# Values by matmuls of 512 columns, and the AdaLN rows' loads moved ahead in a hybrid decoder layer

## The chip, the core and the metric

The kernel runs on one core of a Trainium2 chip. The metric is the device time of one execution in microseconds. Engines are named as in the profile: PE (TensorE) with its weight loads PEld, DVE (VectorE), ACT (ScalarE), POOL (GpSimd) and SP (SyncE, which issues most DMAs here).

## The reference

One decoder layer, one sequence of 512 tokens, width 2048, in float32. A mixing layer runs two groups of heads side by side: stick-breaking attention with 8 heads of 128, and an RG-LRU recurrence with 8 heads of 128; then comes a squared-ReLU MLP of width 8192. Each of the two sub-layers is normalised and modulated by six vectors (shift, scale and gate twice) that come from the conditioning vector c.

```python
mod = silu(c) @ w_ada + b_ada            # six vectors of 2048
h   = rmsnorm(x, g) * (1 + scale) + shift
q, k, v, xr, xg = split(h @ w_in)        # 3 x 1024 and 2 x 1024 columns
z = q k^T * 128**-0.5                    # per head, strictly causal
A[t,s] = sigmoid(z_ts) * prod_(s<j<t) (1 - sigmoid(z_tj))
attn = A v
lru  = scan(a, u) * gelu(xg)             # a, u from sigmoid gates of conv(xr)
x = x + gate * (concat(rmsnorm(attn), rmsnorm(lru)) @ w_out)
x = x + gate * (relu(h2 @ w_mlp_in)**2 @ w_mlp_out)
```

The names here are shortened; the sums are those of the reference.

## The kernel before, in words

Activations lie transposed: 16 chunks k of 128 features by 512 tokens. Every product is made from two halves of each operand, a high part in the reduced format fp32r and the rest: `mm3` issues high x high, low x high and high x low (L259, L262, L263) into one PSUM bank of 128x512. Weights come in by SP (L236, tile `wr`), ACT rounds them to the high part (L244, `wh`) and DVE subtracts (L122, `wl`). There are eight PSUM banks: four `mm`, three `z`, one `o`.

The stages that matter, in order of time:

- The first query-key group is fused with the first V group (from about 105 to 200 us): for each k, 12 matmuls of 128x512 into the `mm` banks and the V matmuls of heads 0 to 3 (`v_mm`, L470 to L472) into the `z` and `o` banks. For V the tokens are the stationary operand, a block of 128 at a time, and the weights are the moving one.
- `qk_group(2)`, then `v_group(4)` (V of heads 4 to 7 into the `mm` banks, about 256 to 317 us), `qk_group(4)` and `qk_group(6)`, then `xg_group(0)`, the first half of the recurrence's gate input (from about 436 us).
- Between their matmuls, generators put pieces of other work: `pair(h)` is attention for heads h and h + 1 (scores, the shares of the stick with two triangular constants at L652, values), `gates` and `scans` are the recurrence (L587 to L595: exponential and square on ACT, sums, roots on ACT, product and a scan on DVE), and `adas` builds the modulation vectors: DVE multiplies a row of w_ada by c and sums it (L211), from an `x` buffer that SP has loaded (L199), and L220 adds bias. Each `yield` gives its spacing in units of the main stream, and `pace` is 3.2 or 1.6 for a row of `adas`.

All instructions are put into one order per engine when the kernel is built, by a scheduler with priorities; an engine then works through its own list without leaving it. A tile that is asked for while its pool is full gets the buffer of an older one, and its first writer waits for the last reader of that.

Two pools matter. `x` has 4 buffers, for AdaLN rows, for the recurrence's temporaries and the gates' operands. `a` has 64 buffers of 128x512, for the normalised activations (two for each of 16 chunks), for the query and key halves, the V halves, the attention outputs and the recurrence's streams `xr_t` and `conv_y`. The evictions of query-key banks (`qk_evac`, ACT at L459, then DVE at L460) and of V banks (`v_evac`, L480 and L481) take two `a` buffers a bank. They are asked for with high priority. The heads' parts of a V bank are read by `values` through the table `vt`; the two buffers of a bank come free when the last of those parts has been read.

Of the kernel before, what the change touches and what calls it, by code (L numbers as in the profile page):

```python
# [12 lines left out]
AF = mybir.ActivationFunctionType  # L13
ALU = mybir.AluOpType
PSUM = bass.MemoryType.PSUM

P = 128
S = 512
D = 2048
NK = D // P  # L20
# [44 lines left out]
def hybrid_layer_kernel(  # L65
# [32 lines left out]
    def T(tag, dt=F32, cols=None):  # L98
        return new(next(split_tag) if tag == "w4" else tag, dt, cols)
# [13 lines left out]
    act = nc.scalar.activation  # L113
    stt = nc.vector.scalar_tensor_tensor
    tt = nc.vector.tensor_tensor
    mm = nc.tensor.matmul

    def f32(ap):
        return ap.bitcast(F32)
# [104 lines left out]
    rows, rows2 = Rows(SC1, SH1), Rows(GT1, SC2, SH2)  # L224
    MID = itertools.cycle(["x"])
# [4 lines left out]
    def weights(src, tag=None, urgent=URGENT, pin=False):  # L230

        n = src.shape[-1] if len(src.shape) == 2 else src.shape[1] * src.shape[2]
        with tc.high_priority(offset=urgent):
            r = T("wr" if tag not in ("w3", "w4", "ts") else "raw")
            dst = r[:, :n] if len(src.shape) == 2 else r[:, :n].rearrange("p (a b) -> p a b", b=src.shape[2])
            dma = nc.sync.dma_start(dst, src)  # L236
            if pin:
                later(dma)
            if tag in ("w4", "ts"):
                both = T(tag, F32R)  # L240
                h, lo = both[:, :S], both[:, S : 2 * S]
            else:
                h, lo = T(tag or "wh", F32R), T(tag or "wl", F32R)
            act(h[:, :n], r[:, :n], AF.Copy)  # L244
            low(lo[:, :n], r[:, :n], h[:, :n])
        return h, lo
# [18 lines left out]
    def blk(o):  # L265
        return slice(o * P, (o + 1) * P)
# [32 lines left out]
    bg, bgl, bg2 = Lane(), Lane(), Lane()  # L299
# [67 lines left out]
    xs, xhl, hT = {}, {}, {}  # L367
# [35 lines left out]
    def weights1(k, halves=(0, 1)):  # L403
        return [weights(w_in[blk(k), XR + i * 512 : XR + (i + 1) * 512], tag="a", urgent=min(k * 28, URGENT), pin=True) for i in halves]
# [6 lines left out]
    w = weights1(0, [0])  # L411
# [4 lines left out]
    for k in range(NK):  # L416
# [18 lines left out]
        for hf in range(2):  # L435
            wh, wl = w[hf]
            for o in range(4):
                mm3(banks[hf * 4 + o], wh[:, blk(o)], wl[:, blk(o)], *xhl[k], k == 0, k == NK - 1)
        w = w_next
    xr_t = []  # L440
    for o in range(8):
        t = T("a")
# [5 lines left out]
    qk, vt, o_t = {}, {}, []  # L448
# [13 lines left out]

    def v_mm(bs, w, k, os=range(4)):

        ah, al = hT[k]
        for o, b in ((o, b) for o in os for b in (o % 2 * 2, o % 2 * 2 + 1)):
            wh, wl = (t[:, o // 2 * 256 : o // 2 * 256 + 256] for t in w)
            out = bs[o][:, (b % 2) * 256 : (b % 2) * 256 + 256]
            st = k == 0 and b % 2 == 0
            mm(out, ah[:, blk(b)], wh, start=st, stop=False, skip_group_check=True)  # L470
            mm(out, al[:, blk(b)], wh, start=False, stop=False, skip_group_check=True)
            mm(out, ah[:, blk(b)], wl, start=False, stop=k == NK - 1, skip_group_check=True)  # L472

    def v_evac(bs, h0, os=range(4)):

        for o in os:
            p, b = o // 2, o % 2
            h, lo = T("a", F32R), T("a", F32R)
            with tc.high_priority(offset=EVAC):
                act(h, bs[o], AF.Copy)  # L480
                tt(out=lo, in0=bs[o], in1=f32(h), op=ALU.subtract)  # L481
            for j in range(2):
                for hd in range(2):
                    c = slice(j * 256 + hd * P, j * 256 + (hd + 1) * P)
                    vt[(h0 + 2 * p + hd, 2 * b + j)] = (h[:, c], lo[:, c])


    banks = [bank(t) for t in BANKS]
    for k in range(NK):
        if k + 2 < NK:  # L490
            prep2(k + 2)
        wh, wl = weights(src_qk[blk(k), :, : 2 * P])
        for o in range(4):
            mm3(banks[o], wh[:, blk(o)], wl[:, blk(o)], *hT[k], k == 0, k == NK - 1)
        v_mm(banks[4:], weights(src_v(k, 0, 4)), k)
    qk_evac(banks[:4], 0)
    v_evac(banks[4:], 0)

    def qk_group(h0, begun=(0, None)):
# [3 lines left out]
    def v_group(h0):  # L503
        bs = [bank("mm") for _ in range(4)]
        load, step = lambda k: weights(src_v(k, h0, 4)), lambda k, w, os: v_mm(bs, w, k, os)
        for k in range(NK - 2):
            step(k, load(k), range(4))
            tick()
        ending(load, step, range(NK - 2, NK), lambda o: v_evac(bs, h0, [o]))
# [88 lines left out]
    def lru_out(o0):  # L598
        for o in range(o0, o0 + 4):
            act(xg_t[o], xg_t[o], AF.Gelu_apprx_tanh)  # L600
        yield 1.0
        for o in range(o0, o0 + 4):
            g = xg_t[o]
            tt(out=g, in0=conv_y[o], in1=g, op=ALU.mult)
            add_square(acc_l, g, T("n"), o == 0)
            yield 1.0
# [89 lines left out]
    def adas(m):  # L696
        for j in range(NK):
            if tags2[0] is MID:
                rows2.row(m, j, MID)
                yield pace[0]  # L700
            else:
                for q in range(2):
                    rows2.row(m, j, LATE, q)
                    yield pace[0] / 2
        ready.add(m)

    pace = [3.2]
# [26 lines left out]
    def xg_group(o0, tags):  # L734
        bs = [bank(t) for t in tags]

        def evac(b):
            t = T("a")
            copy(b, t, bs[b])
            xg_t[o0 + b] = t  # L740

        group(bs, range(NK), lambda k: w_in[blk(k), XG + o0 * P : XG + (o0 + 4) * P], lambda k: hT[k], evac)
# [4 lines left out]
    bg.drain()  # L747
    bg.add(pair(2))
    bg2.add(adas(GT1), adas(SC2), adas(SH2))
    v_group(4)  # L750
    bg.drain()
# [14 lines left out]
    bg.add(attn_mix())  # L766
    bgl.add(lru_out(0))
    tags2[0] = LATE
    rows2.load(5, LATE)
    xg_group(4, BANKS[4:])  # L770
    bg.drain()
# [46 lines left out]
    def out_evac(outs, g, tok, held=None):  # L818
# [35 lines left out]
        out=gm2, in0=mods[:, SC2 * NK : (SC2 + 1) * NK], scalar=1.0, in1=vec[:, C_GMLP : C_GMLP + NK],  # L854
# [226 lines left out]
    def strassen(src, acts, after=None, pre=None, before=None, js=range(8)):  # L1081

        bs = [bank(next(turn)) for _ in PRODUCTS]
        if pre:
            n, ts = pre
            with tc.high_priority(offset=SETE):
                for b, t in zip(bs, ts):
                    act(b, t, AF.Copy)
                for b, t in zip(bs[5:], load_pre(n, (5, 6), nc.scalar)):
                    act(b, t, AF.Copy)  # L1090
        if before:
            loaded[0] = before()
        for j in js:
            w, a = operands(src(j)), acts(j)
            for b, (an, wn) in zip(bs, PRODUCTS):
                (ah, al), (wh, wl) = a[an], w[wn]
                for i in range(2):
                    out, st = b[:, q_(i)], j == js[0] and i == 0 and not pre
                    kw = dict(skip_group_check=True)
                    mm(out, wh[:, blk(i)], ah, start=st, stop=False, **kw)  # L1100
                    mm(out, wh[:, blk(i)], al, start=False, stop=False, **kw)  # L1101
                    mm(out, wl[:, blk(i)], ah, start=False, stop=j == js[-1], **kw)  # L1102
            if after:
                after(j)
            tick()
        return bs
# [108 lines left out]
    for g in range(1, NG):  # L1215
# [3 lines left out]
        bs = strassen(lambda j: w_pair[j][:, :, g * 512 : (g + 1) * 512], acts_in, last, js=range(KP)[:: -1 if g == 1 else 1])  # L1219
# [35 lines left out]
    for i, (n, ps) in enumerate(parts):  # L1255
# [15 lines left out]
        bs = strassen(src, acts_out, after, nxt, before, ps)  # L1271
        nxt = loaded[0]
        if n not in left:
# [11 lines left out]
            with tc.high_priority(offset=SETW):  # L1285
                for k, tok, q in quarters(n, *qs):
                    t = x2[k][:, tok]
# [5 lines left out]
        else:  # L1293
            with tc.high_priority(offset=SETE):
                for j, b in enumerate(bs):
                    t = T("a")
# [14 lines left out]
    for p in final:  # L1311
        t = T("a", F32R)
# [154 lines left out]
```

## Time and profile before

| | us |
|---|---|
| median of 3 runs | 2001.72 (1998.12 to 2003.39) |
| the profiled execution | 2001.01 |
| its span, first to last instruction | 1999.3 |
| PE busy | 1947.6 (97%) |
| DVE busy | 1761.3 (88%) |
| ACT busy | 1073.4 (54%) |

The mean granted clock is 0.995. A matmul's busy time in the profile (0.28 us for 256 columns, 0.40 for 512) is longer than its step to the next start, since matmuls are pipelined; its cost in a stream is the distance of starts. In a timeline row stand the start, the duration, the engine, the line, the operation, the written and the read tile, the sizes, and in brackets the idle time before it with what ended it. A row of waits names the engine, tile and line that waited, whom it waited for, the total, the number of waits and the longest.

### The profile page before, as it was taken

How to read it: one execution, taken by the hardware profiler on the slowest of the kernel's cores; microseconds unless marked ns; L12 is line 12 of the kernel's file. 1: busy time of each engine (PE TensorE's matmuls, PEld its weight loads, DVE VectorE, ACT ScalarE, POOL GpSimd, SP SyncE). 2: the span in 40 equal slices, each digit the busy share in tenths (PEclk: the TensorE clock that was granted, in tenths of full speed). 3: DMA queues.
4: the chain of work that ended last, by engine and by line, in shares of the span. 5: the costliest groups of instructions: out<-in, count | busy, mean ns of one | idle time of the engine just before them, and what ended most of it. 6: DMA issues, size and time to landing. Idle time of an engine off the chain costs nothing. (4 is left out here: it accounts for less than half of the span.)

```text
span 1999.3 us, 37951 instructions
## 1 busy us (share of the span) xinstructions
PE 1947.6 (97%) x14532; PEld 1836.1 (92%) x14532; DVE 1761.3 (88%) x2971; ACT 1073.4 (54%) x1572; POOL 193.6 (10%) x307
## 2 busy tenths in 40 slices
PE   8999999999999998999999999999999999999997
PEld 6789898788888898999999999999999999999996
DVE  8998786888998599999999999999879879878996
ACT  5443564786533386555556555555445645556552
POOL 0000000000000000111211211200110210211100
PEclk9999999999999999999999999999999999999998
DMA  9896655646779543766766765756567668679653
GB/s 365 305 319 213 201 169 183 188 140 213 228 251 362 183 144 113 236 211 196 227 201 191 227 204 187 232 170 219 190 232 270 226 246 287 215 253 346 225 196 111
DMA packets 205241, 443.56 MB, mean 222 GB/s; under 512 B 20481, under 2 KB 42113, under 8 KB 205058
## 3 DMA queue, kind: packets, MB, share of 16 engines
q1 hardware_dynamic: 176338, 356.58, 54.3%
q0 software_dynamic: 23680, 77.61, 10.4%
q10 hardware_dynamic: 5040, 6.93, 1.0%
q8 instruction: 114, 1.87, 0.4%
q14 instruction: 69, 0.57, 0.1%
HBM read 376.30 MB, written 64.75 MB: 221 GB/s over the span
## 5 line engine op out<-in xcount | busy, mean ns | idle before, releaser
L1100 PE MATMUL ps_mm<-a,w 128*128 128x256 f32 x1696 | 468.3, 277 | 3.0 <-DVE a L1112 1.2
L1102 PE MATMUL ps_mm<-a,w 128*128 128x256 f32 x1696 | 468.5, 277 | 0.4 <-DVE w L122 0.3
L1101 PE MATMUL ps_mm<-a,w 128*128 128x256 f32 x1696 | 468.3, 276 | 0.3 <-DVE a L122 0.3
L1070 ACT ACTIVATE w<-ts 128x1024 fp32r<-128x1024 f32 x244 | 258.4, 1059 | 276.2 <-DVE ts L1066 246.5
L1102 PE MATMUL ps_z<-a,w 128*128 128x256 f32 x1304 | 361.6, 278 | 7.0 <-DVE w L122 6.7
L1100 PE MATMUL ps_z<-a,w 128*128 128x256 f32 x1304 | 361.6, 278 | 3.8 <-DVE a L1116 1.7
L1101 PE MATMUL ps_z<-a,w 128*128 128x256 f32 x1304 | 360.9, 277 | 0.1
L122 DVE TENSOR_TENSOR w<-ts,w 128x1024 fp32r<-128x1024 f32 x244 | 298.4, 1223 | 54.7 <-PE ps_mm L1101 17.7
L1100 PEld LDWEIGHTS ps_mm<-a,w 128*128 128x128 f32 x1696 | 318.3, 188 | 4.3 <-issue 2.6
L1102 PEld LDWEIGHTS ps_mm<-a,w 128*128 128x128 f32 x1696 | 318.4, 188 | 1.2 <-DVE w L122 1.0
L1101 PEld LDWEIGHTS ps_mm<-a,w 128*128 128x128 f32 x1696 | 318.5, 188 | 0.7 <-DVE a L122 0.7
L122 DVE TENSOR_TENSOR w<-raw,w 128x768 fp32r<-128x768 f32 (+1 forms) x296 | 268.5, 908 | 37.1 <-ACT w L244 21.8
L1064 ACT ACTIVATE w<-raw 128x768 fp32r<-128x768 f32 x244 | 204.4, 838 | 168.4 <-issue 77.2
L1102 PEld LDWEIGHTS ps_z<-a,w 128*128 128x128 f32 x1304 | 245.6, 189 | 8.4 <-DVE w L122 8.3
L1100 PEld LDWEIGHTS ps_z<-a,w 128*128 128x128 f32 x1304 | 245.6, 188 | 5.4 <-issue 2.2
L1101 PEld LDWEIGHTS ps_z<-a,w 128*128 128x128 f32 x1304 | 245.6, 188 | 0.6 <-DVE a L122 0.6
L244 ACT ACTIVATE wh<-wr 128x512 fp32r<-128x512 f32 (+1 forms) x184 | 113.1, 618 | 151.3 <-PE ps_mm L262 62.4
L1058 DVE TENSOR_TENSOR ts<-raw 128x512 f32<-128x512 f32 x244 | 167.6, 688 | 14.1 <-DMA raw<-in_w_mlp_out_dram 13.6
L259 PE MATMUL ps_mm<-a,wh 128*128 128x512 f32 x448 | 176.3, 394 | 3.8 <-ACT wh L244 2.2
L263 PE MATMUL ps_mm<-a,wl 128*128 128x512 f32 x448 | 175.4, 392 | 0.8 <-DVE wl L122 0.6
L262 PE MATMUL ps_mm<-a,wh 128*128 128x512 f32 x448 | 174.8, 390 | 0.0
L211 DVE SCALAR_TENSOR_TENSOR x<-x,cb 128x1024 f32<-128x1024 f32 x108 | 131.8, 1224 | 25.0 <-DMA x<-in_w_adaT_dram 24.9
(336 smaller groups left out, 4156.7 us busy)
## 6 DMA issues: line engine op xcount, KB each, us to landing
raw<-in_w_mlp_out_dram SPq DMA_DIRECT2D x124, 512.0 KB, 4.7
raw<-in_w_mlp_in_dram SPq DMA_DIRECT2D x120, 512.0 KB, 3.9
x<-in_w_adaT_dram SPq DMA_DIRECT2D x108, 512.0 KB, 5.9
wr<-in_w_in_dram SPq DMA_DIRECT2D x160, 256.0 KB, 3.4
tt<-in_w_adaT_dram SPq DMA_DIRECT2D x52, 512.0 KB, 6.4
part<-a POOLq DMA_DIRECT2D x84, 256.0 KB, 3.9
a<-part SPq DMA_DIRECT2D x84, 256.0 KB, 6.4
prod<-a POOLq DMA_DIRECT2D x63, 256.0 KB, 5.7
```

The source lines that it names most:

```text
L122: tt(out=out, in0=full, in1=f32(high), op=ALU.subtract)
L211: ins = stt(out=t, in0=t, scalar=1.0, in1=cb[q_], op0=ALU.mult, op1=ALU.mult, accum_out=self.ga[:, q_ : q_ + 1],)
L244: act(h[:, :n], r[:, :n], AF.Copy)
L259: first = mm(out, wh, ah, start=start, stop=False, **kw)
L262: mm(out, wh, al, start=False, stop=False, **kw)
L263: mm(out, wl, ah, start=False, stop=stop, **kw)
L1058: tt(out=t[:, : 2 * HT].rearrange("p (a b) -> p a b", a=2), in0=r[:, HT : 3 * HT].rearrange("p (a b) -> p a b", a=2), in1=r[:, q_(0)].unsq ...
L1064: act(h, r[:, HT:], AF.Copy)
L1070: act(h, t, AF.Copy)
L1100: mm(out, wh[:, blk(i)], ah, start=st, stop=False, **kw)
L1101: mm(out, wh[:, blk(i)], al, start=False, stop=False, **kw)
L1102: mm(out, wl[:, blk(i)], ah, start=False, stop=j == js[-1], **kw)
```

## The change

First, `v_mm` and `v_evac`. A bank held two blocks of tokens for two heads: 256 columns by one stationary block, then 256 by the next. Now a bank holds one block of tokens for all four heads of the group: one matmul of 512 columns in the place of two of 256. A matmul's two operands, their sum over k and the number of evictions stay.

Second, `adas` in the stages up to `xg_group(0)`: a row's two loads were issued where its sums stand, and then came one spacing; now the loads come first, then 0.6 of the spacing, the sums, and 0.4. A loop before the last stage uses up what is loaded and not summed yet.

```diff
--- before.py
+++ after.py
@@ -462,27 +462,21 @@
 
     def v_mm(bs, w, k, os=range(4)):
 
-        ah, al = hT[k]
-        for o, b in ((o, b) for o in os for b in (o % 2 * 2, o % 2 * 2 + 1)):
-            wh, wl = (t[:, o // 2 * 256 : o // 2 * 256 + 256] for t in w)
-            out = bs[o][:, (b % 2) * 256 : (b % 2) * 256 + 256]
-            st = k == 0 and b % 2 == 0
-            mm(out, ah[:, blk(b)], wh, start=st, stop=False, skip_group_check=True)
-            mm(out, al[:, blk(b)], wh, start=False, stop=False, skip_group_check=True)
-            mm(out, ah[:, blk(b)], wl, start=False, stop=k == NK - 1, skip_group_check=True)
+        (ah, al), (wh, wl) = hT[k], w
+        for b in os:
+            mm(bs[b], ah[:, blk(b)], wh, start=k == 0, stop=False)
+            mm(bs[b], al[:, blk(b)], wh, start=False, stop=False)
+            mm(bs[b], ah[:, blk(b)], wl, start=False, stop=k == NK - 1)
 
     def v_evac(bs, h0, os=range(4)):
 
-        for o in os:
-            p, b = o // 2, o % 2
+        for b in os:
             h, lo = T("a", F32R), T("a", F32R)
             with tc.high_priority(offset=EVAC):
-                act(h, bs[o], AF.Copy)
-                tt(out=lo, in0=bs[o], in1=f32(h), op=ALU.subtract)
-            for j in range(2):
-                for hd in range(2):
-                    c = slice(j * 256 + hd * P, j * 256 + (hd + 1) * P)
-                    vt[(h0 + 2 * p + hd, 2 * b + j)] = (h[:, c], lo[:, c])
+                act(h, bs[b], AF.Copy)
+                tt(out=lo, in0=bs[b], in1=f32(h), op=ALU.subtract)
+            for hd in range(4):
+                vt[(h0 + hd, b)] = (h[:, blk(hd)], lo[:, blk(hd)])
 
 
     banks = [bank(t) for t in BANKS]
@@ -696,8 +690,10 @@
     def adas(m):
         for j in range(NK):
             if tags2[0] is MID:
+                rows2.load(2, MID)
+                yield 0.6 * pace[0]
                 rows2.row(m, j, MID)
-                yield pace[0]
+                yield 0.4 * pace[0]
             else:
                 for q in range(2):
                     rows2.row(m, j, LATE, q)
@@ -766,6 +762,8 @@
     bg.add(attn_mix())
     bgl.add(lru_out(0))
     tags2[0] = LATE
+    while rows2.tiles:
+        bg2.next()
     rows2.load(5, LATE)
     xg_group(4, BANKS[4:])
     bg.drain()
```

In the diff, `blk(b)` is the b-th block of 128 columns, `act` is an ACT instruction, `tt` and `stt` are DVE instructions, and `mm` is a matmul with its output, stationary and moving operand. Three lines further down in the changed kernel are numbered lower by 6 (L580 is the square that was L586, L581 was L587, L584 the root L590, L587 was L593, L589 the scan L595); V's matmuls are L467 to L469 and its evictions L476 and L477.

PE, in the fused stage, a piece of the V matmuls of one k. Before, from the second block of the first bank on:

```order
L470 MATMUL ps_z_1056<-wh_1093,a_985 128x256
L471 MATMUL ps_z_1056<-wh_1093,a_986 128x256
L472 MATMUL ps_z_1056<-wl_1094,a_985 128x256
L470 MATMUL ps_z_1057<-wh_1093,a_985 128x256
L471 MATMUL ps_z_1057<-wh_1093,a_986 128x256
L472 MATMUL ps_z_1057<-wl_1094,a_985 128x256
```

Now, the first bank and the second:

```order
L467 MATMUL ps_z_1056<-wh_1093,a_985 128x512
L468 MATMUL ps_z_1056<-wh_1093,a_986 128x512
L469 MATMUL ps_z_1056<-wl_1094,a_985 128x512
L467 MATMUL ps_z_1057<-wh_1093,a_985 128x512
L468 MATMUL ps_z_1057<-wh_1093,a_986 128x512
L469 MATMUL ps_z_1057<-wl_1094,a_985 128x512
```

Of each k's 24 matmuls of 256 columns, 12 of 512 are left, each bank's three together; the banks and the order among them are as they were. PE has 384 rows fewer in all, 14505 and 14121.

DVE, at the end of `qk_group(6)` (heads 6 and 7). `ps_mm_3767` is its fourth bank before, `ps_mm_3379` the same bank now; `x_3936` and `x_3937` hold the recurrence's temporaries now, `x_4324` before. Before:

```order
L460 SCALAR_TENSOR_TENSOR a_4368<-ps_mm_3766,a_4367 128x512
L122 TENSOR_TENSOR wl_4463<-wr_4460,wh_4462 128x512
L460 SCALAR_TENSOR_TENSOR a_4382<-ps_mm_3767,a_4381 128x512
L122 TENSOR_TENSOR wl_4483<-wr_4480,wh_4482 128x512
L362 TENSOR_TENSOR n_2033<-n_2033,tt_4152 128x512
L587 SCALAR_TENSOR_TENSOR x_4324<-n_4371,x_4324 128x512
L122 TENSOR_TENSOR wl_4503<-wr_4500,wh_4502 128x512
L587 SCALAR_TENSOR_TENSOR x_4325<-n_4385,x_4325 128x512
L211 SCALAR_TENSOR_TENSOR x_4392,ga_4389<-x_4392,cb_82 128x1024
```

Now:

```order
L581 SCALAR_TENSOR_TENSOR x_3936<-n_3987,x_3936 128x512
L211 SCALAR_TENSOR_TENSOR x_4007,ga_4092<-x_4007,cb_82 128x1024
L581 SCALAR_TENSOR_TENSOR x_3937<-n_4001,x_3937 128x512
L581 SCALAR_TENSOR_TENSOR x_3937<-n_4063,x_3937 128x512
L220 SCALAR_TENSOR_TENSOR mods<-ga_4092,vec 128x1
L211 SCALAR_TENSOR_TENSOR x_4136,ga_4237<-x_4136,cb_81 128x1024
L587 TENSOR_TENSOR a_3495<-x_3936,a_3495 128x512
L587 TENSOR_TENSOR a_3602<-x_3936,a_3602 128x512
L589 SCALAR_TENSOR_TENSOR a_3495<-a_1034,a_3495 128x512
L589 SCALAR_TENSOR_TENSOR a_3602<-a_1036,a_3602 128x512
L587 TENSOR_TENSOR a_3631<-x_3937,a_3631 128x512
L460 SCALAR_TENSOR_TENSOR a_3998<-ps_mm_3379,a_3997 128x512
```

The fourth bank's eviction (L460) stood between two weight splits, and it now stands behind the second recurrence's sums, two AdaLN rows and the first two scans (L589). On ACT the same bank's L459 moves likewise, from between two weight roundings to behind the roots:

```order
L459 ACTIVATE a_4367<-ps_mm_3766 128x512
L244 ACTIVATE wh_4462<-wr_4460 128x512
L459 ACTIVATE a_4381<-ps_mm_3767 128x512
L244 ACTIVATE wh_4482<-wr_4480 128x512
L361 ACTIVATE tt_4152<-a_4353 128x512
L586 ACTIVATE n_4371<-a_1036 128x512
L585 ACTIVATE a_1038<-a_1038,nspl 128x512
```

and now:

```order
L579 ACTIVATE a_1038<-a_1038,nspl 128x512
L579 ACTIVATE a_1040<-a_1040,nspl 128x512
L1416 ACT_TABLE_LOAD
L580 ACTIVATE n_4001<-a_1038 128x512
L580 ACTIVATE n_4063<-a_1040 128x512
L584 ACTIVATE x_3936<-x_3936 128x512 x2
L584 ACTIVATE x_3937<-x_3937 128x512 x2
L1416 ACT_TABLE_LOAD
L459 ACTIVATE a_3997<-ps_mm_3379 128x512
L244 ACTIVATE wh_4118<-wr_4116 128x512
```

Its tile `a_3997` now waits for the scan that reads `a_1034` (the recurrence's first stream), and `a_3998`, which DVE writes, for the scan that reads `a_1036`; before, the two tiles of this bank had no reader of that kind to wait for.

PE, from the start of `xg_group(0)`, whose fourth bank is the one that this eviction sets free (`ps_mm_4400` before, `ps_mm_4012` now). Before:

```order
L259 MATMUL ps_mm_4399<-a_985,wh_4403 128x512
L262 MATMUL ps_mm_4399<-a_986,wh_4403 128x512
L263 MATMUL ps_mm_4399<-a_985,wl_4404 128x512
L262 MATMUL ps_mm_4397<-a_999,wh_4462 128x512
L263 MATMUL ps_mm_4397<-a_998,wl_4463 128x512
L259 MATMUL ps_mm_4400<-a_985,wh_4403 128x512
L262 MATMUL ps_mm_4400<-a_986,wh_4403 128x512
L263 MATMUL ps_mm_4400<-a_985,wl_4404 128x512
L259 MATMUL ps_z_4419<-a_4320,a_4367 128x512
```

Now:

```order
L259 MATMUL ps_mm_4011<-a_1069,wh_4098 128x512
L262 MATMUL ps_mm_4011<-a_1070,wh_4098 128x512
L263 MATMUL ps_mm_4011<-a_1069,wl_4099 128x512
L259 MATMUL ps_mm_4012<-a_985,wh_4015 128x512
L262 MATMUL ps_mm_4012<-a_986,wh_4015 128x512
L263 MATMUL ps_mm_4012<-a_985,wl_4016 128x512
L259 MATMUL ps_z_4031<-a_3932,a_3983 128x512
L262 MATMUL ps_z_4031<-a_3933,a_3983 128x512
L263 MATMUL ps_z_4031<-a_3932,a_3984 128x512
L259 MATMUL ps_z_4032<-a_3932,a_3983 128x384
```

The fourth bank's first matmuls stood behind those of the third for the first weight tile; they now stand behind three weight tiles' matmuls on three banks, and the scores (`ps_z`) still come right after them.

SP's loads of AdaLN rows (L199) stand, up to `xg_group(0)`, in the same or nearly the same places among the weight loads: at the end of `v_group(4)`, for instance, one pair goes ahead of one weight load. DVE's sums (L211) move by a few rows against their neighbours. From `xg_group(4)` on the order of every engine is the same in both kernels.

## The prediction

> **What bounds the kernel now.** I read the page's busy shares first, then windows by stage, then who made TensorE wait in the stages that the change touches.
>
> ```profile
> PE 1947.6 (97%) x14532; PEld 1836.1 (92%) x14532; DVE 1761.3 (88%) x2971; ACT 1073.4 (54%) x1572; POOL 193.6 (10%) x307
> ...
> 105.00:135.00 30.00, 30.00 (x189) 27.17 (x188) 29.26 (x54) 13.81 (x24) 0.00 (x0) 1.00 0.95 337
> 135.00:175.00 40.00, 40.00 (x258) 36.52 (x258) 40.00 (x74) 14.33 (x23) 0.00 (x0) 1.00 0.72 234
> 175.00:200.00 25.00, 25.00 (x157) 22.59 (x156) 15.88 (x24) 9.85 (x18) 0.00 (x0) 1.00 0.67 220
> 256.86:317.06 60.20, 59.49 (x474) 58.55 (x473) 43.16 (x74) 33.49 (x48) 0.00 (x0) 1.00 0.55 171
> ```
>
> A window row gives the stretch, its length, the busy time of PE, PEld, DVE, ACT and POOL, the granted clock, the DMA share and GB/s. In the first V group (fused with the first query-key group, to 200) PE is busy for all 95 us. DVE is full to 175 but PE never waits for it, and it falls to 15.88 of 25 at the end, so its queue is worked off before the stage closes. In the second V group PE loses 0.7 of 60.2 us. So both V groups are bound by PE's own matmuls: what is saved there shortens the run. The same question for everything up to the last query-key group, in the view of waits (time, times, longest):
>
> ```profile
> PE ps_mm L259 <- ACT a L382: 2.7, 1, 2.7
> PE ps_z L652 <- ACT tt L642: 2.1, 3, 1.3
> PE ps_z L652 <- DVE tt L122: 1.2, 3, 0.8
> PE ps_mm L259 <- DVE a L460: 1.0, 2, 0.8
> PE ps_mm L470 <- DVE a L460: 0.7, 1, 0.7
> PE ps_mm L259 <- DVE a L481: 0.6, 1, 0.6
> PE ps_mm L263 <- DVE wl L122: 0.6, 1, 0.6
> ```
>
> PE has little to give back: these seven sorts of wait are all above 0.5 us, 8.9 us in 370, and the first, before the V groups, isn't touched.
>
> **V by 512 columns.** The shape's price stands side by side in the fused stage, where V (L470) and query-key matmuls (L259) alternate, and V's again in the second group:
>
> ```profile
> 109.96 0.28 PE L470 MATMUL ps_z<-wh,a 128*128 128x256 f32 x1
> ...
> 112.83 0.40 PE L259 MATMUL ps_mm<-a,wh 128*128 128x512 f32 x1
> ...
> 115.58 0.28 PE L470 MATMUL ps_z<-wh,a 128*128 128x256 f32 x1
> ...
> 256.86 0.28 PE L470 MATMUL ps_mm<-wh,a 128*128 128x256 f32 x1
> ...
> 258.65 0.28 PE L470 MATMUL ps_mm<-wh,a 128*128 128x256 f32 x1
> ```
>
> Between the first two starts are 24 matmuls, 2.87 us or 0.1196 each; between the next two 12 of 512 columns, 2.75 us or 0.229 each; between the last two 15, 0.1193 each. Starts count here, since the durations overlap. All V matmuls, 768 of 256, take 768 x 0.1196 = 91.9 us; 384 of 512 take 384 x 0.229 = 87.9. The 512 form runs at 0.227 in unbroken stretches (PE rows below, 436.11 to 437.24: 5 steps, 0.226 each), which gives 86.8 to 87.2. Gain 4.0 to 5.1; I take **4.4 us**. The 384 weight loads that go lie under the matmuls (PEld isn't waited for) and give nothing of their own. The evictions stay 4 + 4 per group, of the same 128x512.
>
> The TensorE page of the Trainium skill ("TensorE: Matmul & The Clock Gate", section "Back-to-back issue gap") gives a warm gap of columns over 2.4 GHz plus 2.5 ns: joining two matmuls would save 2.5 ns, 1.0 us over 384. The rows above show 0.1196 x 2 - 0.229 = 10 ns a pair, so here the rows decide; the sum by the page is among the rivals.
>
> **AdaLN loads ahead.** What DVE and PE lose on these loads:
>
> ```profile
> DVE x L211 <- DMA x<-in_w_adaT_dram: 20.8, 13, 4.3
> ...
> 315.72 1.23 DVE L211 SCALAR_TENSOR_TENSOR x<-x,cb 128x1024 f32<-128x1024 f32 x1 [0.71 <-DMA x<-in_w_adaT_dram]
> ...
> 327.96 1.23 DVE L211 SCALAR_TENSOR_TENSOR x<-x,cb 128x1024 f32<-128x1024 f32 x1 [4.26 <-DMA x<-in_w_adaT_dram]
> ...
> 320.91 0.48 PE L259 MATMUL ps_mm<-a,wh 128*128 128x512 f32 x1 [0.56 <-DVE a L481]
> ...
> 391.01 0.50 PE L652 MATMUL ps_z<-tt,ntri 128*128 128x512 f32 x1 [1.35 <-ACT tt L642]
> ```
>
> DVE waits 20.8 us between 100 and 700, but PE feels almost none: the 4.26 us wait has no PE wait behind it. And in the order of the changed kernel SP issues these loads at almost the same places; DVE's rows (L211) are what moves, some a few places later. One pair of loads at the end of the second V group goes ahead of one weight load; the two waits at 313 and 315.72, which stand among the V evictions, should shrink, and with them the 0.56 at 320.91 (0.7 counted by starts): **-0.7**. Before the scores' shares at 391.01 one L211 row moves off the chain that ends in L642; of the 1.35 I take **-0.5**. Bounds of this part: +1 (a load that now holds an x buffer longer) to -3 (all waits below 2.7 in the list that end on DVE or behind it). No work is added: as many DMAs, as many L211.
>
> **The buffers that V now holds.** Before, a V eviction's two `a` tiles hold two heads for two token blocks; when the first pair of heads is done, four of the eight are free. Now each tile holds four heads of one block, and all eight stay until the fourth head. The pool has 64. By the orders, and by what each instruction waits for, one eviction is hit: the last bank of the query-key group of heads 6 and 7. Its two tiles now become those that the first and second scan (L595) of the second recurrence set free. On DVE it moves behind twelve rows, on ACT behind two exponentials, two squares, four roots and two table loads. How that runs, from rows of before:
>
> ```profile
> 438.90 0.64 ACT L586 ACTIVATE n<-a 128x512 f32<-128x512 f32 x1
> 439.42 0.73 ACT L585 ACTIVATE a<-a,nspl 128x512 f32<-128x512 f32 x1
> ...
> 444.00 1.28 ACT L1418 ACT_TABLE_LOAD   x1
> ```
>
> ```profile
> 438.76 0.68 DVE L460 SCALAR_TENSOR_TENSOR a<-ps_mm,a 128x512 fp32r<-128x512 f32 x1
> 439.36 0.68 DVE L122 TENSOR_TENSOR wl<-wr,wh 128x512 fp32r<-128x512 f32 x1
> 439.96 0.69 DVE L362 TENSOR_TENSOR n<-n,tt 128x512 f32<-128x512 f32 x1
> 440.57 0.69 DVE L587 SCALAR_TENSOR_TENSOR x<-n,x 128x512 f32<-128x512 f32 x1
> ...
> 442.37 1.22 DVE L211 SCALAR_TENSOR_TENSOR x<-x,cb 128x1024 f32<-128x1024 f32 x1
> ...
> 447.06 1.22 DVE L595 TENSOR_TENSOR_SCAN a<-a,a 128x512 f32<-128x512 f32 x1
> ```
>
> ```profile
> 436.11 0.39 PE L259 MATMUL ps_mm<-a,wh 128*128 128x512 f32 x1
> ...
> 437.24 0.39 PE L263 MATMUL ps_mm<-a,wl 128*128 128x512 f32 x1
> ...
> 438.30 0.50 PE L259 MATMUL ps_mm<-a,wh 128*128 128x512 f32 x1 [0.26 <-DVE a L460]
> ...
> 442.09 0.28 PE L263 MATMUL ps_z<-a,a 128*128 128x256 f32 x1
> ...
> 455.56 0.49 PE L652 MATMUL ps_z<-tt,ntri 128*128 128x512 f32 x1 [0.46 <-ACT tt L642]
> ...
> 457.94 0.50 PE L652 MATMUL ps_z<-tt,ntri 128*128 128x512 f32 x1 [0.80 <-DVE tt L122]
> ```
>
> In before's clock: without the eviction at 438.76 the weight split stands at 438.76 and L362 at 439.36. Then L362 0.6 (439.96 to 440.57), L587 three times 0.6, L211 twice 1.2, L220 0.1, three L593 at 0.6 like the other rows of 512, and two scans at 1.2: 9.1 us, 448.5. Two of the L587 wait for ACT, which ends their squares at about 442.1 and 442.6 (a square, two exponentials of 0.7 and a table load of 1.3 from 438.4 on, one square earlier than in before): some 0.4 more. The eviction starts at about 448.9 and ends at 449.5. PE meanwhile does the other three banks for three weight tiles, 27 matmuls from 436.11 on, 6.2 us with 0.5 of small waits, done at 442.75. It then idles until 449.5: **6.75 us**, where before it lost 0.6.
>
> Late next are the scores queued behind that bank's matmuls, now done at 452.1, not 442.3. From the last scores row (442.09) to the second half of the shares (457.94) before took 15.85; the table load that held ACT there until 445.3 is over by then, as are the roots, so I take 14.3: 466.4. Before's PE stands at the same amount of work, eight matmuls further on, at 457.94 + 8 x 0.2285 = 459.8. Net **+6.6 us**; with the 14.3 between 12.7 and 15.9 it is 5 to 8.2, and the next heads' scores may add to 9.
>
> A pause also costs clock:
>
> ```profile
> 101.00:104.50 3.50, 3.50 (x11) 2.67 (x10) 3.50 (x7) 0.72 (x1) 0.00 (x0) 0.52 0.97 354
> ```
>
> Behind the wait of 2.7 us on L382 (the first row of PE's list, it ends at 100.0) the clock is 0.52 for 3.5 us: up to 1.8 us lost. Here it falls on matmuls that end before the shares' chain does, so I count 0. (Part 1 of the same page of the Trainium skill, on the clock gate, says that an idle window of about 3.4 us halves the clock; the two rows agree, at a shorter pause.)
>
> **Sum.** The profiled execution took 2001.0 (its span 1999.3, 1.7 around it), 0.7 below the median of the runs: 2001.0 - 4.4 - 1.2 + 6.6 = **2002.0 us**, no change that can be told; this kernel's measurement tells about 0.3%, 6 us.
>
> **Rivals.** (1) *The eviction's wait costs nothing*: 2001.0 - 5.6 = 1995.4, at the edge of faster. For it: the 27 matmuls are 6.2 us of cover, and DVE may reach the list's head sooner than in before. Against: two scans and two L211 alone are 4.8 us, and before the eviction at 438.76 was already what PE waited for. (2) *Slower, by a late load*: the L211 third of the way down that list needs a load which SP issues only at about 437.7, when an L211 has freed its x buffer.
>
> ```profile
> 437.67 0.33 SPq L199 DMA_DIRECT2D x<-in_w_adaT_dram  x1
> ...
> DMA to landing us min/median/max: 3.5/5.2/10.5
> ```
>
> My chain wants it at 443.4, 5.7 us later. At the longest landing it comes at 448.2, 4.8 late; all behind it, the scans, the eviction and PE, waits too, and the clock's 1.8 is then in the open: +6.6 + 4.8 + 1.8 - 5.6 = +7.6, 2008.6. It decides from a landing of about 9 us. (3) *V saves only 1.0*, an equal rate per column: 2005.4. (4) *The loads ahead do what they say* and take 3 us off: 2000.2.
>
> **Numbers.** Forecast 0.60; rival 1 0.16 (half of it below -0.3%); rival 2 0.10; rival 3 0.06; rival 4 0.08. The forecast's own range is 1998 to 2006; with the first two rivals all but the outer tenths lies in 1995.5 to 2006.8. Faster: 0.08 of rival 1 and 0.05 of tails of the forecast and rival 4; slower: rival 2's 0.10.
>
> **What would show it.** V rows at 0.228 spacing in both groups and both ending together about 4.4 us earlier; one PE wait of 6 to 7 us on L460 some 440 us in, three banks' matmuls ahead of it, and the scans directly before that L460 on DVE; a window of about half clock behind it. Wrong if that wait is under 3 us, if PE gains waits for L122 in the fused stage (DVE then bounds it), or if L211's waits fall from 20.8 to below 10 and PE's waits with them.

## The result, and the profile after

The changed kernel takes 2013.22 us (median of 4 runs, 2012.3 to 2015.46), before 2002.39 (4 runs, 1998.12 to 2003.39): a ratio of 1.0055, 95% interval 1.0042 to 1.0068. That is 11 us slower, where 2002.0 was forecast and 2006.8 was the upper end of the range.

What makes TensorE wait between 100 and 700 us in the changed kernel (time, times, longest; L467 is V's first matmul, L477 V's eviction on DVE, L646 the shares):

```profile
PE ps_mm L259 <- DVE a L460: 7.2, 3, 6.6
PE ps_mm L259 <- DVE a L477: 3.1, 2, 2.3
...
PE ps_mm L467 <- DVE a L460: 2.7, 3, 1.6
PE ps_z L646 <- DVE tt L122: 2.4, 1, 2.4
```

Before, the same four kinds were 1.0, 0.6 (L481), 0.7 (L470) and 1.2 us. Three places have grown most: the entry and the exit of the second V group (L467 and L477, at 254 to 259 and at 317 to 319 us) and the last query-key bank with the shares behind it. The third in PE's timeline, first matmul of the gate product, the stall, the second half of the shares, the start of the last shares:

```profile
436.00 0.39 PE L259 MATMUL ps_mm<-a,wh 128*128 128x512 f32 x1
...
449.41 0.79 PE L259 MATMUL ps_mm<-a,wh 128*128 128x512 f32 x1 [6.63 <-DVE a L460]
...
468.57 0.50 PE L646 MATMUL ps_z<-tt,ntri 128*128 128x512 f32 x1 [2.40 <-DVE tt L122]
...
487.52 0.39 PE L646 MATMUL ps_z<-tt,ntri 128*128 128x512 f32 x1
```

The stall lies where the forecast had it, to 0.1 us: it ends at 449.4. (The clock times of before and after agree at 436 because the 3.4 us that are won up to V's last matmul are lost again by 3.3 us between there and the gate product.) What follows it was not forecast. The windows behind the three pauses (length, PE busy, granted clock, DMA share, GB/s):

```profile
319.30:322.70 3.40, 3.39 (x8) 0.52 0.87 228
449.40:452.50 3.10, 3.09 (x8) 0.53 0.02 8
468.50:472.50 4.00, 3.93 (x15) 0.61 0.57 177
```

A fourth place does not stand out among the waits. Ahead of the shares at 389 us PE waits 1.7 us, 1.35 before, and the clock is half from 391 to 394. The run with both parts, halves and loads 0.9 ahead (below) issues the same 45 matmuls there behind the same pause. The first twelve start at the same distances, to 0.02 us; then the clock stays up there, and the 45 take 1.25 us less. PE's row and window in the changed kernel, then the window in that run:

```profile
389.25 0.50 PE L646 MATMUL ps_z<-tt,ntri 128*128 128x512 f32 x1 [1.72 <-ACT tt L636]
391.00:394.00 3.00, 3.00 (x12) 0.50 0.21 49
```

```profile
388.00:391.00 3.00, 2.92 (x17) 1.00 0.15 41
```

And DVE ahead of the shares' second half (the L122 row that writes `tt`):

```profile
464.12 1.23 DVE L211 SCALAR_TENSOR_TENSOR x<-x,cb 128x1024 f32<-128x1024 f32 x1 [1.64 <-DMA x<-in_w_adaT_dram]
...
465.88 1.23 DVE L211 SCALAR_TENSOR_TENSOR x<-x,cb 128x1024 f32<-128x1024 f32 x1 [0.52 <-DMA x<-in_w_adaT_dram]
...
467.03 1.49 DVE L122 TENSOR_TENSOR tt<-tt,tt 128x1280 fp32r<-128x1280 f32 x1
```

Executions differ by some 4 us in when the first V group starts, 108 to 112 us, so stages are compared by distances between four PE starts: the first V matmul, the last V matmul of the second group, the first matmul of the gate product, and the start of the last shares. Before: 109.96, 316.94, 436.11, 477.18. Worked out so from each profiled execution (us; the last column is the ratio of the timed runs to those of before, with its 95% interval):

| kernel | to the end of V | to the gate product | to the last shares | ratio to before |
|---|---|---|---|---|
| before | 207.0 | 119.2 | 41.1 | |
| changed | 203.6 | 122.5 | 51.5 | 1.0055 (1.0042 to 1.0068) |
| V part alone | 204.2 | 118.5 | 52.7 | 1.0030 (1.0016 to 1.0044) |
| the same again | 204.3 | 118.0 | 52.4 | one run |
| loads ahead alone | 205.9 | 123.5 | 41.0 | 1.0011 (1.0001 to 1.0021) |
| V part, evictions in halves | 201.9 | 117.9 | 40.9 | 0.9974 (0.9963 to 0.9985) |
| both, evictions in halves | 201.5 | 122.5 | 41.1 | 0.9996 (0.9984 to 1.0008) |
| 256 columns, buffers held | 206.8 | 118.2 | 52.1 | 1.0052 (1.0037 to 1.0066) |
| halves in the second group only | 200.9 | 118.2 | 40.8 | 0.9974 (0.9962 to 0.9987) |
| both, halves, loads 0.9 ahead | 203.9 | 117.8 | 40.8 | 0.9975 (0.9964 to 0.9986) |
| held, 22 idle matmuls in the stall | 205.0 | 118.2 | 48.4 | 1.0033 (1.0021 to 1.0046) |
| held, 26 idle matmuls ahead | 205.8 | 119.0 | 49.0 | 1.0031 (1.0020 to 1.0043) |
| halves in the second, loads 0.9 ahead | 201.4 | 117.4 | 41.1 | 0.9959 (0.9942 to 0.9975) |

The table reads by columns. The third is 41 or 52 (48 to 49 with idle matmuls), the second 117.4 to 119.2 or, with the loads 0.6 ahead, 122.5 to 123.5. Behind the last of the four starts each of these executions takes 1520 to 1524 us to its end, without a pattern by kernel.

### The profile page after: what moved, and what is told of

It reads as the page before. It is cut to its first block, busy times and chain, and to the rows that moved or that the text cites. A ratio compares the mean times of both kernels' runs of the same rounds, so it can differ in the third digit from the quotient of the medians.

```text
span 2010.5 us, 37179 instructions
## 1 busy us (share of the span) xinstructions
PE 1948.0 (97%) x14148; PEld 1821.4 (91%) x14148; DVE 1761.7 (88%) x2971; ACT 1071.5 (53%) x1570; POOL 193.5 (10%) x307
## 3 DMA queue, kind: packets, MB, share of 16 engines
q0 software_dynamic: 23680, 77.61, 10.4%
## 5 line engine op out<-in xcount | busy, mean ns | idle before, releaser
L122 DVE TENSOR_TENSOR w<-ts,w 128x1024 fp32r<-128x1024 f32 x244 | 298.4, 1223 | 58.0 <-PE ps_mm L1099 18.6
L122 DVE TENSOR_TENSOR w<-raw,w 128x768 fp32r<-128x768 f32 (+1 forms) x296 | 268.4, 908 | 38.9 <-ACT w L244 24.3
L1062 ACT ACTIVATE w<-raw 128x768 fp32r<-128x768 f32 x244 | 204.3, 838 | 174.2 <-issue 81.7
L263 PE MATMUL ps_mm<-a,wl 128*128 128x512 f32 x448 | 175.9, 393 | 0.1
L211 DVE SCALAR_TENSOR_TENSOR x<-x,cb 128x1024 f32<-128x1024 f32 x108 | 131.9, 1224 | 37.9 <-DMA x<-in_w_adaT_dram 37.6
```

The costliest lines, as they stand in the source:

```text
L122: tt(out=out, in0=full, in1=f32(high), op=ALU.subtract)
L211: ins = stt(out=t, in0=t, scalar=1.0, in1=cb[q_], op0=ALU.mult, op1=ALU.mult, accum_out=self.ga[:, q_ : q_ + 1],)
L263: mm(out, wl, ah, start=False, stop=stop, **kw)
L1062: act(h, r[:, HT:], AF.Copy)
```

## The experiments

**The two parts apart.** The V part alone keeps `adas` as it was:

```diff
-                rows2.load(2, MID)
-                yield 0.6 * pace[0]
                 rows2.row(m, j, MID)
-                yield 0.4 * pace[0]
+                yield pace[0]
```

(The loop ahead of the last stage falls away with it.)

> The V part alone: matmuls of 512, AdaLN loads where they were before. Theory (two separate costs: the late eviction of the last query-key bank comes from V's buffers, the late evictions around V's second group come from the loads ahead): the gap of about 6.8 us near 445 us stays with its half clock behind it, the gaps near 255 and 318 us are as short as in before (0.9 and 1.4 us); V's matmuls give 5 us; time 2 to 6 us above before. Rival (all of the loss comes from V): about 11 us above before, with the gaps at 255 and 318 us there too. Rival (the loads ahead are what makes that eviction late): no gap at 445 us and 5 us below before.

2009.4 us, by the ratio 6 us above before (3 to 9). The stall is there without the loads ahead, and the exit of V costs 1.2 us of gaps, 1.45 in before. The entry of V is not as short as the theory had it: 3.2 us. PE's waits from 200 to 700 us:

```profile
PE ps_mm L259 <- DVE a L460: 8.1, 3, 5.8
...
PE ps_mm L467 <- DVE a L460: 2.7, 3, 1.5
```

A second trace of the same kernel:

> The V part alone once more, for a second trace of the same program. If the 6.5 us landing of the AdaLN load at 247 us belongs to the program, the gaps at the entry of the second V group are again about 3.2 us; if it is chance, they differ by a us or more. The gap at 445 us stays at 5.5 to 7 us in either case.

2005.4 us in that one run; entry gaps 2.6 us again, the stall 6.9. In both traces the AdaLN row that stands ahead of the entry's evictions is summed 6.5 us after SP issued its load (246.98 to 253.50 and 244.14 to 250.71), in the changed kernel 6.8; in before it was 4.1, with halves 4.5, with 256 columns and held buffers (below) 4.1. So it isn't chance from run to run, but with 0.9 ahead and halves, a kernel without the stall, it is 6.6 too: it isn't the held buffers either. What sets it to about 4.5 or 6.5 stays open; against the 0.5 us of gaps that the entry has with halves, the price is 2 to 2.7 us of V's gain.

The loads ahead alone have the diff of `adas` and the loop, with V by 256:

> The loads ahead alone, V by 256 columns as before. Theory: no gap at 445 us, since four of V's eight buffers come free as before; evictions around V's second group wait on DVE behind sums whose row has not landed: 5 to 6 us of gaps near 259 and 320 us against 2.3 in before, DVE's waits for these loads above 28 us against 20.8 between 100 and 700 us; time 2 to 6 us above before. Rival (V's shorter stages make the loads late, not the loads ahead): gaps and waits as in before, time within 2 us of before.

2003.16 us, 2 us above before (0.2 to 4.2): no stall, and the loss is at V's exit, 4.4 us of gaps there against 1.45, a half clock behind them, and 29.1 us of DVE waits for these loads against 20.8. By gaps and waits the rival falls; the time alone, at the edge of its 2 us, would not decide. The gap at V's entry that the theory had too is not there: 0.5 us, less than in before. The half clock at 391 to 394 us is here as well. The two parts by themselves add up to 8 us, the change has 11; with intervals of 2 to 3 us each, these are not told apart. DVE at that place, then SP's queue (x2: two issues; the row's length includes what lies between them):

```profile
309.83 1.23 DVE L211 SCALAR_TENSOR_TENSOR x<-x,cb 128x1024 f32<-128x1024 f32 x1 [3.86 <-DMA x<-in_w_adaT_dram]
...
310.98 0.69 DVE L122 TENSOR_TENSOR wl<-wr,wh 128x512 fp32r<-128x512 f32 x1
...
317.26 1.23 DVE L211 SCALAR_TENSOR_TENSOR x<-x,cb 128x1024 f32<-128x1024 f32 x1 [3.09 <-DMA x<-in_w_adaT_dram]
...
319.02 0.68 DVE L481 TENSOR_TENSOR a<-ps_mm,a 128x512 fp32r<-128x512 f32 x1
```

```profile
306.00 6.08 SPq L236 DMA_DIRECT2D wr<-in_w_in_dram  x2
312.12 0.93 SPq L199 DMA_DIRECT2D x<-in_w_adaT_dram  x2
```

The chain closes on itself. One pair of loads goes ahead of a weight load on SP, and its sums go ahead of the weight split L122 on DVE. The sums wait 3.86 us for the landing, the split waits behind them, the weight buffer that it frees comes late, SP's next weight load waits for that buffer, and the next AdaLN pair, queued behind on SP, is issued at 312.12. It lands at 317.26, and the third V bank's eviction stands behind its sum. PE waits:

```profile
319.76 0.50 PE L259 MATMUL ps_mm<-a,wh 128*128 128x512 f32 x1 [3.11 <-DVE a L481]
321.65 0.66 PE L259 MATMUL ps_mm<-a,wh 128*128 128x512 f32 x1 [0.93 <-DVE a L481]
```

**The held buffers.** V by 512 columns, each eviction in two halves, so that a buffer again holds two heads for two blocks (against the V part alone):

```diff
-            h, lo = T("a", F32R), T("a", F32R)
-            with tc.high_priority(offset=EVAC):
-                act(h, bs[b], AF.Copy)
-                tt(out=lo, in0=bs[b], in1=f32(h), op=ALU.subtract)
-            for hd in range(4):
-                vt[(h0 + hd, b)] = (h[:, blk(hd)], lo[:, blk(hd)])
+            if b % 2 == 0:
+                pq[:] = [(T("a", F32R), T("a", F32R)) for _ in range(2)]
+            for p in range(2):
+                (h, lo), half = pq[p], slice(p * 256, p * 256 + 256)
+                to = slice(b % 2 * 256, b % 2 * 256 + 256)
+                with tc.high_priority(offset=EVAC):
+                    act(h[:, to], bs[b][:, half], AF.Copy)
+                    tt(out=lo[:, to], in0=bs[b][:, half], in1=f32(h[:, to]), op=ALU.subtract)
+                for hd in range(2):
+                    c = slice(b % 2 * 256 + hd * P, b % 2 * 256 + (hd + 1) * P)
+                    vt[(h0 + 2 * p + hd, b)] = (h[:, c], lo[:, c])
```

> The V part alone with each bank's eviction in two halves of 256 columns, so that a buffer holds two heads for two blocks of tokens as before: 8 evictions in the place of 4 on ACT and on DVE per group. Theory: the eviction of the last query-key bank stands where it stood, no gap at 445 us, V's gain of 5 us stays but for the extra evictions' 0.6 us on DVE and ACT: 3 to 5 us below before. Rival (that gap has another cause than the buffers): a gap of over 3 us there and no gain.

1996.13 us, 5 us below before (3 to 7). No stall; PE's waits from 430 to 490 us are those of before to 0.1 us, and one of 0.3 us on L460 is gone:

```profile
PE ps_z L653 <- DVE tt L122: 0.8, 1, 0.8
PE ps_z L653 <- ACT tt L643: 0.4, 1, 0.4
```

With the loads ahead as well:

> The change with evictions in halves as in the run before. Theory: the gap at 445 us goes, the gaps at 255 and 318 us stay: 7 to 9 us below the change as it is, 1 to 4 us above before. Rival (the costs aren't separate, the loads ahead cost only together with the late eviction): 4 us or more below before.

1999.4 us, not told apart from before, and by the ratios 12 us below the change, more than the 7 to 9 of the theory. The stall is gone, and the exit of V keeps its gaps, here as a wait for a weight split that stands behind the same sums (`PE ps_mm L263 <- DVE wl L122`, 3.1 us once). But the gap at the entry, which the theory kept, is gone (0.2 us by starts; the load is summed 4.2 us after its issue), and no half clock follows the shares at 387 us. The middle column is 122.5 as in the changed kernel, made up differently: the 31st matmul of the next product starts 13.5 us after V's last, in the changed kernel 12.2 and in before 8.6, and the changed kernel has the 1.25 us of half clock on top.

Halves in the second V group only (the edit above, with the whole eviction kept for the first group):

> The V part alone, evictions in halves only in the second V group. Theory A (only the second group's buffers decide, and the gaps of 3.2 us at the entry of the second V group in the run with whole evictions are a late landing of one AdaLN load): gaps at that entry of 0.5 to 3 us by the landing, no gap at 445 us, time within 2 us of the run with both groups in halves, about 1996. Theory B (the first group's held buffers make that entry late): 3 us of gaps there again and 1999 or more.

1993.41 us, the same ratio of 0.9974. So only the second group's buffers decide; the entry's gap is 1.0 us here.

The buffers without the 512 columns: banks as in the changed kernel, by matmuls of 256 (against the V part alone).

```diff
-            mm(bs[b], ah[:, blk(b)], wh, start=k == 0, stop=False)
-            mm(bs[b], al[:, blk(b)], wh, start=False, stop=False)
-            mm(bs[b], ah[:, blk(b)], wl, start=False, stop=k == NK - 1)
+            for p in range(2):
+                c = slice(p * 256, p * 256 + 256)
+                st = k == 0 and p == 0
+                mm(bs[b][:, c], ah[:, blk(b)], wh[:, c], start=st, stop=False, skip_group_check=True)
+                mm(bs[b][:, c], al[:, blk(b)], wh[:, c], start=False, stop=False, skip_group_check=True)
+                mm(bs[b][:, c], ah[:, blk(b)], wl[:, c], start=False, stop=k == NK - 1, skip_group_check=True)
```

> V by 256 columns as before, but each bank holds one block of tokens for four heads, so that all eight buffers stay until the fourth head; loads as before. It takes V's gain away and leaves the held buffers alone. Theory (the held buffers cost by themselves): a gap of 6 to 7 us near 450 us, time 8 to 14 us above before, about 5 us above the V part alone. Rival (the shorter V stages are what makes things late): no such gap, within 2 us of before.

2010.21 us, 10 us above before (7 to 13), and the third column 52.1 - 41.1 = 11.0 us longer. PE's waits from 430 to 490, and the window behind the stall:

```profile
PE ps_mm L259 <- DVE a L460: 6.6, 1, 6.6
PE ps_z L649 <- DVE tt L122: 2.8, 1, 2.8
```

```profile
447.00:452.00 5.00, 4.65 (x18) 0.64 0.16 54
```

So the held buffers alone make the whole loss of the third column.

**The half clock and the rows ahead of the shares.** The same kernel with idle matmuls, whose result nobody reads; with an offset of -150 the order puts 22 of 28 just before the fourth bank's first matmul, the other six later, up to 470 us:

```diff
     bg.add(pair(6))
+    with tc.high_priority(offset=-150):
+        idle = bank("o")
+        for _ in range(28):
+            mm(idle, hT[0][0][:, blk(0)], hT[0][0], start=True, stop=True)
     xg_group(0, BANKS[:4])
```

> The run with 256 columns and held buffers, and in it 22 or more idle matmuls of 512 columns (their result is read by nobody) just before the fourth bank's first matmul, 5 us of work in the gap of 6.8 us near 447 us. DVE and ACT keep their order there: two AdaLN rows still stand ahead of the second half that the shares wait for. Theory (half clock behind the gap stands in the open): no half clock at 448 to 451 us, from the start of the gate product to the last shares 1 to 2 us less than in the run without idle matmuls. Rival (as predicted, the half clock is hidden by the shares' chain): the same distance within 0.5 us.

2008.35 us; the third column is 48.4, 3.7 shorter. PE's waits from 430 to 490 and the same window:

```profile
PE ps_mm L259 <- DVE a L460: 1.5, 1, 1.5
PE ps_z L649 <- DVE tt L122: 0.5, 1, 0.5
```

```profile
447.00:452.00 5.00, 3.52 (x20) 1.00 0.32 107
```

The clock stays up. The fourth bank's three matmuls and the twelve of the scores take 2.7 us here, 4.2 with the half clock. From the end of the stall to DVE's last sum for the shares (L636) it takes 460.05 - 448.53 = 11.52 us, with the half clock 460.01 - 447.35 = 12.66: 1.1 us of it stood in the open. The rest of the 3.7 is more than the theory had. The two L211 ahead of the shares' second half wait 0.6 us for their loads here, 2.65 there (1.5 us at that half). And behind that half no second half clock follows: the 21 steps from its first matmul take 3.45 us here, 4.85 there, which is 1.4; four of the idle matmuls run behind them, and from that half to the last shares this run is 1.0 shorter.

With 26 idle matmuls and an offset of 0 they stand among the first weight tile's matmuls:

> As the run before, but 26 idle matmuls among the first weight tile's matmuls of the gate product; by the order DVE now has no AdaLN row between the scores' last sums and the second half for the shares. Theory (those two rows, whose loads land late, are what the shares wait for): the wait of about 3 us near 467 us falls to 1.5 us or less and the distance from the start of the gate product to the last shares is 2 to 4 us below that with held buffers alone. Rival (the shares' chain itself is that long): the wait stays at 2.5 us or more once the half clock is gone.

2007.87 us, the third column 49.0, 3.1 below that with held buffers alone. DVE has no AdaLN row between the last sum and the shares' second half here, and PE's wait for that half is gone from the list of 430 to 490 us (longest from 200 to 700: 0.2). A gap of 2.1 us remains and brings a half clock again (0.72 in that window): the same fifteen matmuls take 4.3 us, 1.6 more than in the run before. By the times the two runs with idle matmuls and the one without aren't told apart; the distances tell them.

**How far ahead.** Both parts, halves, and 0.9 of a spacing in the place of 0.6:

```diff
-                yield 0.6 * pace[0]
+                yield 0.9 * pace[0]
                 rows2.row(m, j, MID)
-                yield 0.4 * pace[0]
+                yield 0.1 * pace[0]
```

> The change with evictions in halves, the loads only 0.9 of a spacing ahead in the place of 0.6 (0.1 after the sums). At the end of the second V group this puts loads and sums back to where they stand without the loads ahead: behind the fourth weight load on SP, between the evictions on DVE. Theory (the loss of the loads ahead is made at that one place): gaps there of 1 to 1.5 us in the place of 4.4, and 1995 to 1998, about 3 us below the run with 0.6. Rival (the loads ahead cost everywhere): still 1999 to 2001.

1995.1 us. At V's exit one wait is left, 1.0 us against 3.1, and the middle column is 117.8. The 31st matmul of the next product starts 8.7 us after V's last, 4.8 earlier than with 0.6, and the two kernels keep this distance up to the gate product: the 4.7 us of the column were made at that one place, by which row stands ahead of the split and the evictions. That the loads are ahead isn't in itself the cause. The gap at V's entry is back, 2.5 us, which is why the first column has 203.9.

The two best pieces together:

> The two best pieces together: V by 512 columns with evictions in halves in the second group only, and loads 0.9 of a spacing ahead. Theory (the loads ahead are worth nothing where they don't cost): 1993 to 1997, ratio 0.997 to 0.998 like the V part with halves alone. Rival (what they save at DVE shows once nothing eats it): 1991 or less, ratio 0.996 or below.

1993.03 us, 0.9959 (0.9942 to 0.9975), 8 us below before and 19 below the change, by the ratios. This is the version to keep. The ratio lies just inside the rival's bound, but its interval holds the theory's values too: whether the 0.9 adds to the halves can't be told.

## Why the prediction was wrong

The sum was -4.4 - 1.2 + 6.6. By the three columns the changed kernel stands at -3.4 + 3.3 + 10.4 = +10.3; the profiled execution ended 11.3 above that of before.

- **V by 512 columns: the size was right, a part was given back.** The first group shows it alone: its last matmul starts 84.1 us behind its first in every kernel with 512 columns and 87.05 with 256. That is 2.95 for half of V's matmuls, above the 2.2 of the forecast: V's step at 0.227, the lower end of what the working had, and the query-key matmuls between them also step at 0.227 instead of 0.229. With halves the first column is 5.1 to 6.1 shorter than before in four kernels, and 3.0 in the fifth, whose entry to the second group was late. In the change 2.3 us more than before go at the second group's entry, where PE meets evictions that stand on DVE behind an AdaLN sum whose load is late. The working treated V's groups as bound by PE alone and did not price this entry. That PE comes 3 us earlier is not enough for it: it does so in the four kernels with halves too, and there the entry costs 0.2 to 1.0. The gap formula of the Trainium skill ("TensorE: Matmul & The Clock Gate", section "Back-to-back issue gap") would give, as an estimate, 1.0 us for both groups, which was rival 3; 2.95 in one rules that out. The section itself calls the formula the isolated gap, not the spacing in a stream.
- **The loads ahead: the sign was wrong.** The step "SP issues these loads at almost the same places ... the two waits at 313 and 315.72 should shrink" counted the pair that moved as a gain. Its sums moved too, ahead of a weight split, and through the weight buffers that delayed the next pair, whose sum stands ahead of the third eviction: 0.7 saved became 3.3 to 4.7 lost (second column, with and without). The rows for this were in the order. What failed was to take a load's place on SP for its landing, and not to follow the moved sum into the split behind it. The -0.5 for the shares at 391 did not come either. By starts the waits of their two halves are 1.5 and 0.3 us before, 1.9 and 0.3 in all five kernels with loads ahead. In two of the five, the change and the loads ahead alone, a half clock follows that costs 1.25; why not in the other three stays open. In the changed kernel the exit costs 3.6, this half clock 1.25, and some 1.5 are won back elsewhere in the column.
- **The held buffers: mechanism, place and stall right, the sum after it too small.** 6.75 us of stall were forecast; by starts it is 6.8 in the changed kernel (6.63 in the row) and 6.0 to 6.9 in the other traces that have it. The term was 6.6 and measured 10.4 to 11.6. Two steps failed. "It falls on matmuls that end before the shares' chain does, so I count 0": among the first matmuls behind the stall are the scores that start this chain. The half clock costs them 1.3 us in the changed kernel, and the idle matmuls show 1.1 us of such a loss arriving at the shares; a second half clock behind the shares' wait costs 1.4. And the 14.3 us from the scores to the shares' second half had no place for the two L211 that the order puts directly ahead of that half: measured 468.57 - 453.32 = 15.3, and PE waits 2.4 us where before it waited 0.8. These are 1.3 + 1.0 + 1.4 = 3.7 of the 3.8 that the term lacks. With the clock up and the loads landed the same stage costs 48.4 - 41.1 = 7.3, with up to 1.4 of it the six later idle matmuls: the 6.6 was the price of the stall without its sequel.
- **The rivals.** The late load behind an L211 (rival 2) was the right kind of loss, but the load named there was in time: the sum at 443.48 waited for nothing. The lateness stood at other L211: at V's entry, at its exit and ahead of the shares. Rival 1's 6.2 us of cover were there, and the eviction came 6.8 us behind them. Rival 4 had the wrong sign.
- **The range** took the held buffers at 5 to 9 and the loads at -3 to +1. Both terms were outside, on the same side. (The waits that the text names for the -3 add up to 4.1 in its list, so this bound does not follow from them.)
- **The signs.** The wait of 6 to 7 us on L460, the scans ahead of it and the half clock behind it all came, and none of the signs of being wrong did. They tested the stall, which was right, and not what followed it.

## What to carry to other kernels

When a layout is changed, ask how long each buffer is now held, and look in the orders of the other engines for the instruction that is pushed behind something long: here four more buffers of 64 cost 11 us, twice the 5 to 6 that the wider matmul saves, and evicting in halves gives the saving without the price. A stall is priced with its sequel: the clock behind it, and the chain that starts late and may meet other queues. A DMA wait on an engine with nobody waiting behind it is free (before, 4.26 us on DVE at 328 us without a wait of PE) until an eviction or a weight split is ordered behind it (3.86 and 3.09 us in the run with loads ahead alone); so place such rows by what stands behind them.

## What the runs showed of the hardware

How long a pause is needed for the clock to fall isn't one number here. A pause is counted as what PE's step takes above its usual length, a loss against the same matmuls in a kernel whose clock stays up, or against steps of 0.227. After a pause of 1.6 us (the first run with idle matmuls) nothing followed. After 1.9 us ahead of the shares at 389 us the clock fell to 0.50 in two kernels, 1.25 us lost each, and stayed at 1.00 in three, with the same matmuls behind it. After 2.1 us 1.6 were lost, after 2.6 to 3.4 us ahead of the shares 1.4 in all four traces, after 6.0 to 6.9 us 1.3 to 1.5: a longer pause did not cost more. The Trainium skill ("TensorE: Matmul & The Clock Gate", Part 1, on the HAM clock gate) has a free-running window of about 3.4 us. That the effect of the same pause varies would fit a window that runs free, but no run here shows where its windows lie, and the short pauses that sufficed are shorter than a whole one.
